# Causal convolution by Karatsuba products: input transposes moved from TensorE to DMA, a fourth accumulation pair, products and sums reordered

## Chip, cores, metric

One core of one Trainium2 chip. The metric is the device time of one launch in microseconds; a run's mean granted TensorE clock (the clock that the chip allowed, 1 being full speed) is given where it matters.

## The reference

```python
# x: (8, 4096, 512) float32, kernel: (8, 512, 512) float32
for k in range(8):
    shifted = x if k == 0 else concat([zeros(B, k, D), x[:, :-k, :]], axis=1)
    out += matmul(shifted, kernel[k])
```

Eight taps, each a 512 x 512 matrix. The kernel splits time in groups of eight and applies a Karatsuba-like scheme three times over: 27 products of a 128 x 512 by 512 x 512 matrix take the place of 64 for each iteration of eight time steps, at the price of sums of inputs (on VectorE) and of results. There are 32 such iterations.

## The kernel before

Each iteration has three nodes, MID, LO and HI, of nine products each. The kernel transposes the input (XT) and loads XT, or sums of it, as the stationary operand (on the page of before, 3,456 weight loads of 128*128 from D and XT). In the profile lines, D stands for the sums and differences of transposed inputs that the prep functions make on VectorE (D1, D2, D4 and so on), pp for an accumulation pair in PSUM, ts and ms for ScalarE's copies of such pairs, y for an output tile.

```python
    xpool = ctx.enter_context(tc.tile_pool(name="x", bufs=2))
    ppool = ctx.enter_context(tc.tile_pool(name="p", bufs=3, space=PSUM))   # accumulation pairs
    tpool = ctx.enter_context(tc.tile_pool(name="t", bufs=2, space=PSUM))   # transposes
    # ... cut ...
    def transpose_x(xin, h, q):                # 8 TensorE transposes and one ScalarE copy
        pt = tpool.tile([P, 2, D], bf, name="pt")
        for j in range(2):
            for c in range(DC):
                nc.tensor.transpose(pt[:, j, c * P:(c + 1) * P],
                                    xin[:, 2 * q + j, c * P:(c + 1) * P], ident)
        nc.scalar.copy(out=XT[:, 4 * h + 2 * q:4 * h + 2 * q + 2, :], in_=pt)
    # ... cut ...
    def node_u(i, a):       # U: one product, then a ScalarE copy within the pair n.q
    def node_a(n):          # A: two products onto n.q, then the ScalarE copy ts
    def node_v(n, b_):      # V: one product to a pair, then the VectorE sum pp with ts
    def node_l(n, b_):      # L: the two last products onto that pair, then ms (ScalarE) or y (VectorE)
    # ... cut: bodies; i is the iteration, a the node, b_ the pair ...
    for k, (i, a) in enumerate(order):
        # ... cut ...
        if a == MID:
            for q in range(2):
                transpose_x(xi[1], 1, q)       # high half of this iteration's input
        if nxt:
            new = node_u(*nxt)
        node_l(cur, 0)
        if nxt:
            node_a(new)
        if a == MID:
            prep_lo_c(); prep_hi_a()           # input sums on VectorE
        elif a == LO:
            prep_d27()
            if not last:
                for q in range(2):
                    transpose_x(xi[0], 0, q)   # low half of the next input
                prep_m()
        elif not last:
            prep_lo_a(); prep_lo_b()
        node_l(cur, 1)
        if nxt:
            node_v(new, 0); node_v(new, 1)
        # ... cut: prep_hi_b, prep_hi_c or prep_d21 ...
```

## Time and profile before

| | before |
|---|---|
| time, median of 7 runs | 1097 us (1094.4 to 1097.9) |
| profiled span, mean clock | 1091.3 us, 0.944 |
| busy TensorE / VectorE / ScalarE | 81% / 73% / 35% |
| start of the first A product | 88.4 us |
| one iteration | 31.25 us |

In 30 of the 31 iterations that have a wait of 2.37 or 2.38 us for D, the granted clock was 0.50 to 0.79 in the 2 us behind it; it was 1.00 behind each of the seven waits for D of 1.13 to 1.24 us.

### The profile page before, as it was taken

The page shows a single profiled execution, that of the slowest core. Times are in us where ns is not written, and L with a number is a line of the kernel's source. Part 1 is how long each engine was busy: PE and PEld are TensorE (multiplying, and loading weights), DVE is VectorE, ACT ScalarE, POOL GpSimd, SP SyncE. Part 2 cuts the span into 40 slices and gives each one's busy share as a digit, 9 for nine tenths or more (in the row PEclk, how much of TensorE's full clock was granted, in tenths as well). Part 3 has the DMA queues.
Part 4 walks back from the last instruction along what each step waited for, and adds up shares of the span by engine and source line. Part 5 has one row for each costly group of instructions (what it writes and reads, how often), then busy time and mean ns, then how long its engine had stood idle before and what let it go on. Part 6 is the DMA issues. An engine that isn't in the chain of part 4 may idle for free. (4 is left out here: it accounts for less than half of the span.)

```text
span 1091.3 us, 11294 instructions
## 1 busy us (share of the span) xinstructions
PE 879.9 (81%) x4432; PEld 406.5 (37%) x4518; DVE 799.4 (73%) x954; ACT 377.5 (35%) x461; POOL 42.9 (4%) x86
## 2 busy tenths in 40 slices
PE   3007888888988888889888888898888888988886
PEld 2003333334443343444333433443334334434342
DVE  2875777777777777787777777877787778777876
ACT  2555233233333233333232333332333333323322
POOL 3000000000000000000000000000000000000000
PEclk9999998999999899999998999999899999989999
DMA  8231343334333433343244233432442334234412
GB/s 207 79 116 39 97 116 98 95 97 116 94 97 100 116 97 97 96 116 88 86 116 116 97 97 97 116 92 82 116 116 97 97 97 116 83 91 116 114 73 84
DMA packets 32436, 110.76 MB, mean 101 GB/s; under 512 B 3472, under 2 KB 3472, under 8 KB 32384
## 3 DMA queue, kind: packets, MB, share of 16 engines
q0 software_dynamic: 9728, 34.54, 18.1%
q1 hardware_dynamic: 22656, 75.51, 17.5%
q8 instruction: 35, 0.57, 0.2%
q14 instruction: 17, 0.14, 0.0%
HBM read 77.46 MB, written 67.11 MB: 132 GB/s over the span
## 5 line engine op out<-in xcount | busy, mean ns | idle before, releaser
L186 PE MATMUL pp<-w,D 128*128 128x512 bf16 x3242 | 789.7, 400 | 112.1 <-DVE D L80 98.1
L186 PEld LDWEIGHTS <-D 128*128 128x128 bf16 x3328 | 329.6, 102 | 561.7 <-DVE D L80 139.1
L80 DVE TENSOR_TENSOR pp<-pp,ts 128x1024 f32<-128x1024 f32 x192 | 226.1, 1223 | 86.1 <-PE pp L186 76.7
L80 DVE TENSOR_TENSOR D<-D 128x512 bf16<-128x512 bf16 (+3 forms) x353 | 242.5, 731 | 2.2
L80 DVE TENSOR_TENSOR y<-pp,ms 128x1024 f32<-128x1024 f32 x128 | 156.0, 1219 | 104.1 <-PE pp L186 101.8
L80 DVE TENSOR_TENSOR D<-XT 128x512 bf16<-128x512 bf16 (+3 forms) x226 | 155.1, 722 | 84.0 <-ACT XT L107 84.0
L214 ACT COPY ts<-pp 128x1024 f32<-128x1024 f32 x96 | 97.2, 1013 | 341.0 <-PE pp L186 336.6
L107 ACT COPY XT<-pt 128x1024 bf16<-128x1024 bf16 x132 | 127.4, 1019 | 107.3 <-PE pt L105 106.2
L207 ACT COPY pp<-pp 128x512 f32<-128x512 f32 x96 | 55.8, 581 | 155.7 <-PE pp L186 155.7
L186 PE MATMUL pp<-w,XT 128*128 128x512 bf16 x128 | 34.1, 384 | 79.1 <-DVE w L80 54.3
L230 ACT COPY ms<-pp 128x1024 f32<-128x1024 f32 x64 | 64.8, 1013 | 69.7 <-PE pp L186 54.5
L105 PE MATMUL pt<-ident,xin 128*128 128x128 bf16 x1056 | 72.2, 223 | 14.0 <-DMA xin<-in_x_dram 13.4
L105 PEld LDWEIGHTS <-xin 128*128 128x128 bf16 x1056 | 66.5, 100 | 29.6 <-issue 13.6
L92 POOL DMA_DIRECT2D xin<-in_x_dram x64 | 33.9, 529 | 984.4 <-PE pt L105 984.4
L186 PEld LDWEIGHTS <-XT 128*128 128x128 bf16 x128 | 12.3, 96 | 85.7 <-issue 73.8
L80 DVE TENSOR_TENSOR mid<-wt 128x1024 f32<-128x1024 f32 (+1 forms) x12 | 18.9, 1574 | 10.0 <-DMA wt<-in_kernel_dram 10.0
L176 ACT CAST w<-mid 128x512 bf16<-128x512 f32 x20 | 12.1, 605 | 25.6 <-DVE mid L80 25.6
L80 DVE TENSOR_TENSOR w<-mid 128x512 bf16<-128x512 f32 x20 | 13.1, 688 | 0.4
L177 ACT ACTIVATE w<-mid 128x512 bf16<-128x512 f32 x20 | 12.5, 625 | 0.0
L80 DVE TENSOR_TENSOR w<-wt 128x512 bf16<-128x512 f32 x16 | 10.3, 683 | 0.0
L177 ACT ACTIVATE w<-wt 128x512 bf16<-128x512 f32 x16 | 10.0, 624 | 0.0
L176 ACT CAST w<-wt 128x512 bf16<-128x512 f32 x16 | 9.6, 601 | 0.0
(13 smaller groups left out, 21.0 us busy)
## 6 DMA issues: line engine op xcount, KB each, us to landing
out_dram<-y SPq DMA_DIRECT2D x128, 512.0 KB, 2.6
xin<-in_x_dram POOLq DMA_DIRECT2D x64, 512.0 KB, 5.0
wt<-in_kernel_dram SPq DMA_DIRECT2D x8, 1024.0 KB, 4.9
xin<-in_x_dram POOLq DMA_DIRECT2D x16, 60.0 KB, 6.7
```

Of the source, the lines that this page charges most:

```text
L80: nc.vector.tensor_tensor(out=o, in0=a, in1=b, op=op)
L92: nc.gpsimd.dma_start(out=xin, in_=xr[:, K * i + 4 * h:K * i + 4 * h + 4, :])
L105: nc.tensor.transpose(pt[:, j, c * P:(c + 1) * P], xin[:, 2 * q + j, c * P:(c + 1) * P], ident)
L107: nc.scalar.copy(out=XT[:, 4 * h + 2 * q:4 * h + 2 * q + 2, :], in_=pt)
L176: nc.scalar.copy(out=W[a, b_, LO][:, c], in_=V[:, 1])
L177: nc.scalar.mul(out=W[a, b_, HI][:, c], in_=V[:, 0], mul=-1.0)
L186: nc.tensor.matmul(bank, lhsT=comp[:, c * P:(c + 1) * P], rhs=w[:, c, :], start=start and c == 0, stop=c == DC - 1, skip_group_check=True)
L207: nc.scalar.copy(out=n.q[:, 0], in_=n.q[:, 1])
L214: nc.scalar.copy(out=n.ts, in_=n.q)
L230: nc.scalar.copy(out=ms[b_], in_=p)
```

## The change

The intent: take the transposes off TensorE and off PSUM. The two PSUM tiles that they held (pt, two of 128x1024 bf16) go, a fourth pair of accumulators (pp, 128x1024 f32) comes, and with four pairs the first product of a node can be issued two nodes ahead. Sums move one slot earlier, and the transposes are issued long before their readers.

```diff
-    ppool = ctx.enter_context(tc.tile_pool(name="p", bufs=3, space=PSUM))
-    tpool = ctx.enter_context(tc.tile_pool(name="t", bufs=2, space=PSUM))
+    ppool = ctx.enter_context(tc.tile_pool(name="p", bufs=4, space=PSUM))
...
-    def transpose_x(xin, h, q):
-        (8 transposes, 1 copy)
+    def transpose_x(xin, h):
+        nc.sync.dma_start_transpose(
+            out=XT[:, 4 * h:4 * h + 4, :].rearrange("p j (c m) -> p (j c) m", m=P),
+            in_=xin.rearrange("p j d -> p (j d)"))
...
     xi = [load_x(0, 0), load_x(0, 1)]
-    for q in range(2):
-        transpose_x(xi[0], 0, q)
+    transpose_x(xi[0], 0)
     prep_m()
-    prep_lo_a()
-    prep_lo_b()
+    prep_d4(LO)
     prep_d21()
+    prep_d41_d42(LO)
+    transpose_x(xi[1], 1)
+    prep_d4(HI)
+    xi = [load_x(1, 0), load_x(1, 1)]
     (the weights' loads and sums follow here, as before)
...
     for k, (i, a) in enumerate(order):          # new order, written out
+        if a == MID and not last:
+            transpose_x(xi[0], 0)
+        node_l(cur, 0, LO); node_l(cur, 0, HI); node_e(cur, 0)
+        if nxt: node_a(nxt)
+        MID: prep_d421(LO)   LO: prep_m(), prep_d4(LO)   HI: prep_d21(), prep_d41_d42(LO)
+        if nxt: node_v(nxt, 0); node_v(nxt, 1)
+        MID: prep_d41_d42(HI), prep_d27()   LO: prep_d421(HI)   HI: prep_d4(HI)
+        node_l(cur, 1, LO)
+        if k + 2 < len(order): nodes.append(node_u(*order[k + 2]))
+        node_l(cur, 1, HI); node_e(cur, 1)
+        if a == LO and not last:
+            transpose_x(xi[1], 1)
+            if i + 2 < NIT: xi = [load_x(i + 2, 0), load_x(i + 2, 1)]
```

More of the change, by code (lines that the diff above doesn't have):

```diff
@@ L80, in tt @@
         nc.vector.tensor_tensor(out=o, in0=a, in1=b, op=op)
-    for _ in range(3):
+    for _ in range(4):
         pw = ppool.tile([P, 2, D], f32, name="pp")
@@ L99, in load_x @@
         return xin
-    def transpose_x(xin, h, q):
-        pt = tpool.tile([P, 2, D], bf, name="pt")
-        for j in range(2):
-            for c in range(DC):
-                nc.tensor.transpose(pt[:, j, c * P:(c + 1) * P],
-                                    xin[:, 2 * q + j, c * P:(c + 1) * P], ident)
-        nc.scalar.copy(out=XT[:, 4 * h + 2 * q:4 * h + 2 * q + 2, :], in_=pt)
+    def transpose_x(xin, h):
+        nc.sync.dma_start_transpose(
+            out=XT[:, 4 * h:4 * h + 4, :].rearrange("p j (c m) -> p (j c) m", m=P),
+            in_=xin.rearrange("p j d -> p (j d)"))
     def prep_m():
@@ L117, in prep_d27 @@
         tt(D2[:, 4], XT[:, 5], XT[:, 7], ADD)
-    def prep_lo_a():
-        tt(D4[:, 0:4], XT[:, 4:8], XT[:, 0:4], ADD)
-        tt(D41[:, 0], D4[:, 7], D4[:, 0], SUB)
-        tt(D41[:, 1], D4[:, 0], D4[:, 1], SUB)
-    def prep_lo_b():
-        tt(D42[:, 0:2], D4[:, 6:8], D4[:, 0:2], ADD)
-        tt(D42[:, 2:4], D4[:, 0:2], D4[:, 2:4], ADD)
     def prep_d21():
@@ L130, in prep_d21, with prep_d4, prep_d41_d42, prep_d421 @@
         tt(D21[:, 1:4], D2[:, 0:3], D2[:, 1:4], SUB)
-    def prep_lo_c():
-        tt(D421[:, 0], D42[:, 7], D42[:, 0], SUB)
-        tt(D421[:, 1:4], D42[:, 0:3], D42[:, 1:4], SUB)
-    def prep_hi_a():
-        tt(D4[:, 4:8], XT[:, 0:4], XT[:, 4:8], ADD)
-        tt(D41[:, 2:4], D4[:, 3:5], D4[:, 4:6], SUB)
-    def prep_hi_b():
-        tt(D42[:, 4:8], D4[:, 2:6], D4[:, 4:8], ADD)
-    def prep_hi_c():
-        tt(D421[:, 4:8], D42[:, 3:7], D42[:, 4:8], SUB)
+    def prep_d4(h):
+        a, b = (XT[:, 4:8], XT[:, 0:4]) if h == LO else (XT[:, 0:4], XT[:, 4:8])
+        tt(D4[:, 4 * h:4 * h + 4], a, b, ADD)
+    def prep_d41_d42(h):
+        if h == LO:
+            tt(D41[:, 0], D4[:, 7], D4[:, 0], SUB)
+            tt(D41[:, 1], D4[:, 0], D4[:, 1], SUB)
+            tt(D42[:, 0:2], D4[:, 6:8], D4[:, 0:2], ADD)
+            tt(D42[:, 2:4], D4[:, 0:2], D4[:, 2:4], ADD)
+        else:
+            tt(D41[:, 2:4], D4[:, 3:5], D4[:, 4:6], SUB)
+            tt(D42[:, 4:8], D4[:, 2:6], D4[:, 4:8], ADD)
+    def prep_d421(h):
+        if h == LO:
+            tt(D421[:, 0], D42[:, 7], D42[:, 0], SUB)
+            tt(D421[:, 1:4], D42[:, 0:3], D42[:, 1:4], SUB)
+        else:
+            tt(D421[:, 4:8], D42[:, 3:7], D42[:, 4:8], SUB)
     xi = [load_x(-1, 0), load_x(-1, 1)]
     for h in range(2):
-        for q in range(2):
-            transpose_x(xi[h], h, q)
+        transpose_x(xi[h], h)
     tt(D4[:, 5:8], XT[:, 1:4], XT[:, 5:8], ADD)
@@ L154 @@
     xi = [load_x(0, 0), load_x(0, 1)]
-    for q in range(2):
-        transpose_x(xi[0], 0, q)
+    transpose_x(xi[0], 0)
     prep_m()
-    prep_lo_a()
-    prep_lo_b()
+    prep_d4(LO)
     prep_d21()
+    prep_d41_d42(LO)
+    transpose_x(xi[1], 1)
+    prep_d4(HI)
+    xi = [load_x(1, 0), load_x(1, 1)]
     with tc.tile_pool(name="wt", bufs=1) as tp:
@@ L222, with node_l, node_e @@
     ms = {}
-    def node_l(n, b_):
+    def node_l(n, b_, j):
+        product(n.p[b_][:, j], n.s[3][2 * b_ + j], W[n.a, b_, j], False)
+    def node_e(n, b_):
         p = n.p[b_]
-        product(p[:, 0], n.s[3][2 * b_], W[n.a, b_, LO], False)
-        product(p[:, 1], n.s[3][2 * b_ + 1], W[n.a, b_, HI], False)
         if n.a == MID:
@@ L237 @@
     order = [(i, a) for i in range(NIT) for a in (MID, LO, HI)]
-    cur = node_u(*order[0])
-    node_a(cur)
-    node_v(cur, 0)
-    node_v(cur, 1)
+    nodes = [node_u(*order[0])]
+    node_a(nodes[0])
+    node_v(nodes[0], 0)
+    node_v(nodes[0], 1)
+    nodes.append(node_u(*order[1]))
     for k, (i, a) in enumerate(order):
-        nxt = order[k + 1] if k + 1 < len(order) else None
+        cur = nodes[k]
+        nxt = nodes[k + 1] if k + 1 < len(order) else None
         last = i + 1 == NIT
-        if a == MID:
-            for q in range(2):
-                transpose_x(xi[1], 1, q)
-            if not last:
-                xi = [load_x(i + 1, 0), load_x(i + 1, 1)]
-        if nxt:
-            new = node_u(*nxt)
-        node_l(cur, 0)
-        if nxt:
-            node_a(new)
-        if a == MID:
-            prep_lo_c()
-            prep_hi_a()
-        elif a == LO:
-            prep_d27()
-            if not last:
-                for q in range(2):
-                    transpose_x(xi[0], 0, q)
-                prep_m()
-        elif not last:
-            prep_lo_a()
-            prep_lo_b()
-        node_l(cur, 1)
-        if nxt:
-            node_v(new, 0)
-            node_v(new, 1)
-        if a == MID:
-            prep_hi_b()
-        elif a == LO:
-            prep_hi_c()
+        if a == MID and not last:
+            transpose_x(xi[0], 0)
+        node_l(cur, 0, LO)
+        node_l(cur, 0, HI)
+        node_e(cur, 0)
+        if nxt:
+            node_a(nxt)
+        if a == MID:
+            prep_d421(LO)
+        elif not last and a == LO:
+            prep_m()
+            prep_d4(LO)
         elif not last:
             prep_d21()
+            prep_d41_d42(LO)
         if nxt:
-            cur = new
+            node_v(nxt, 0)
+            node_v(nxt, 1)
+        if a == MID:
+            prep_d41_d42(HI)
+            prep_d27()
+        elif a == LO:
+            prep_d421(HI)
+        elif not last:
+            prep_d4(HI)
+        node_l(cur, 1, LO)
+        if k + 2 < len(order):
+            nodes.append(node_u(*order[k + 2]))
+        node_l(cur, 1, HI)
+        node_e(cur, 1)
+        if a == LO and not last:
+            transpose_x(xi[1], 1)
+            if i + 2 < NIT:
+                xi = [load_x(i + 2, 0), load_x(i + 2, 1)]
 _INS = ['x', 'kernel']
```

## The prediction

The sum came to 906 us of span, 912 timed and 918 said, and its terms stand; the cut landing enters it only through the start, where the 29 us for the weights' request count four DMA transposes, of which the trace of before has none. The 9% for slower counts some 4% for rival 2.

> **What bounds the kernel now.** I read the busy shares first, then the clock row and the groups, then one iteration in the timeline, then the waits. The chain that ended last is of little use here: its pieces start only at 1051 us, so it tells the last 3% of the run.
>
> ```profile
> PE 879.9 (81%) x4432; PEld 406.5 (37%) x4518; DVE 799.4 (73%) x954; ACT 377.5 (35%) x461; POOL 42.9 (4%) x86
> ...
> PEclk9999998999999899999998999999899999989999
> ...
> L186 PE MATMUL pp<-w,D 128*128 128x512 bf16 x3242 | 789.7, 400 | 112.1 <-DVE D L80 98.1
> L80 DVE TENSOR_TENSOR pp<-pp,ts 128x1024 f32<-128x1024 f32 x192 | 226.1, 1223 | 86.1 <-PE pp L186 76.7
> L80 DVE TENSOR_TENSOR y<-pp,ms 128x1024 f32<-128x1024 f32 x128 | 156.0, 1219 | 104.1 <-PE pp L186 101.8
> L107 ACT COPY XT<-pt 128x1024 bf16<-128x1024 bf16 x132 | 127.4, 1019 | 107.3 <-PE pt L105 106.2
> L105 PE MATMUL pt<-ident,xin 128*128 128x128 bf16 x1056 | 72.2, 223 | 14.0 <-DMA xin<-in_x_dram 13.4
> ...
> out_dram<-y SPq DMA_DIRECT2D x128, 512.0 KB, 2.6
> xin<-in_x_dram POOLq DMA_DIRECT2D x64, 512.0 KB, 5.0
> ```
>
> Neither engine is full: TensorE is busy 81%, VectorE 73%, they wait for each other in turn (VectorE's sums before TensorE's products, TensorE's products before VectorE's evictions), and the clock row is below 10 in nearly every slice. The two DMA rows give the time to landing of 512 KB. The timeline shows one iteration's worst place:
>
> ```profile
> 513.94 1.06 PE L105 MATMUL pt<-ident,xin 128*128 128x128 bf16 x16
> ...
> 516.10 1.96 DVE L80 TENSOR_TENSOR D<-XT 128x512 bf16<-128x512 bf16 x4 [2.12 <-ACT XT L107]
> 517.98 1.22 DVE L80 TENSOR_TENSOR y<-pp,ms 128x1024 f32<-128x1024 f32 x1
> ...
> 519.11 2.35 DVE L80 TENSOR_TENSOR pp<-pp,ts 128x1024 f32<-128x1024 f32 x2
> 519.25 1.02 PE L186 MATMUL pp<-w,XT 128*128 128x512 bf16 x4 [0.80 <-DVE y L80]
> ...
> 521.37 1.21 DVE L80 TENSOR_TENSOR D<-D 128x2048 bf16<-128x2048 bf16 x1
> ...
> 522.64 8.39 PE L186 MATMUL pp<-w,D 128*128 128x512 bf16 x32 [2.37 <-DVE D L80]
> 523.05 0.15 PEld L186 LDWEIGHTS <-D 128*128 128x128 bf16 x1 [0.28 <-issue]
> ```
>
> VectorE waits 2.12 us for the transposed input, so the eviction y comes late, so TensorE waits for a free accumulation pair (0.80 us), then for the last sum (2.37 us). After that the weight loads come 0.43 us apart (0.15 + 0.28) instead of 0.216: the clock has fallen to half, for some 6 matmuls here and some 14 in another iteration that I looked at. The waits repeat in each of the 32 iterations:
>
> ```profile
> PE pp L186 <- DVE D L80: 98.1, 63, 3.0
> PE pp L186 <- DVE y L80: 24.8, 31, 0.8
> ```
>
> One iteration takes 31.25 us (the same transposes start at 93.3 us in the first and at 499.6 us in the fourteenth: 406.3 / 13). It splits so: 27 products of 4 matmuls. A warm run of 28 matmuls took 6.22 us with about 0.17 us of draining in it, so 0.216 us each, 0.863 a product, 23.3 an iteration. Transposes: two groups of 16, issued over about 0.9 us each, 1.8. Waits: (98.1 + 24.8) / 32 = 3.8. The rest, about 2.3 us, is the half clock (6 to 14 matmuls lose 0.21 us each). Sum 31.2.
>
> [...] The trace of before has no DMA transpose; its plain 512 KB store lands in 2.6 us. [...]
>
> **The change part by part.** *Removed:* 1,056 transposes on TensorE (1.8 us an iteration, on the path) and 132 copies on ScalarE (127.4 us in all; ScalarE is 35% busy, so it gains nothing itself, but the 2.12 us wait of VectorE goes). *Added:* 66 DMA transposes of 512 KB on the SP queue. *Moved:* the first product of a node is issued two nodes ahead, between the two last products of the current one, and sums go one slot earlier. VectorE's work is the same: 18 sums, 6 pp and 4 y per iteration. So the floors are TensorE 23.3 us and VectorE about 23.4 us (the mean busy time in three stretches of 31.3 us is 23.49). Both cannot be met, since they still hand over to each other, so I walk the new order of each engine with measured times. Back to back, VectorE takes 1.14 for pp or y (two pp in 2.35), 1.13 for a 2048 sum, 0.87 for 1536, 0.60 for 1024, 0.33 for 512. TensorE to VectorE or ScalarE costs 0.2 after the last matmul's issue end (0.17 drain), the other way 0.06.
>
> Time 0 is the MID node's start. Each node has nine products: two last ones (b=0), A, A, V, V, a last one, U of the node after next, a last one, 7.8 us unstalled. MID has no y, so VectorE has room: its pp end at 7.1, its sums at 9.1. LO starts at 7.8; its first pair is complete at 9.53. From here VectorE has in a row: y 9.73 to 10.87; D1 and D2 (4 sums, 1.87) to 12.74; D4 low 1.13 to 13.87; two pp to 16.14; D421 high 1.13 to 17.27. TensorE has finished LO at 15.6 and needs D421 high for HI: it waits until 17.35, about 1.75 us. HI then runs unstalled to 25.15 (its pp for the next MID end at about 24.7 and 25.8, in time for 25.2 and later). The ring that repeats is 20 products (17.3 us) plus a VectorE segment of 1.14 + 1.87 + 1.13 + 2.27 + 1.13 + 0.26 = 7.8 us, together 25.1 us. Seven products hide under the segment. A stall of 1.75 us amid dense products should not drop the clock, as the present lone waits of 1.1 us do not. So an iteration goes from 31.25 to 25.1 us.
>
> *The fourth pair:* the second V needs the pair that y(b=0) frees, about 1.5 us after its last product while TensorE has three other products, 2.6 us; U takes the pair freed by the ts copy, 2.6 us after A with 1.25 needed. Neither waits. With three pairs this order would.
>
> *The transposes' deadlines:* the low half is issued behind the y store of HI, about 2.9 us into MID, and is needed at 10.87, so it may take 8 us. The high half is issued behind y of LO at 18.4 and is needed by the D4 high sums at 25.8: 7.4 us, and about 1.2 more before VectorE's slack in MID is gone. [...]
>
> *The start:* now the four first transposes stand ahead of the kernel's weights on the SP queue; before, weights were requested at 0.74 us. The fourth must follow both input loads (5.0 us each) and the first D4 sums. I estimate weights requested near 29 us, the first mid4 sum near 36 instead of 29.8: plus 6 us. The later weight chunks keep their period of 15 us. U of the second node adds 0.9. The first MID node thus starts near 93 + 7 = 100 us.
>
> *Sum:* 100 + 31 x 25.1 + 23.4 (the last iteration lacks the next input's sums and so the stall) + 1.4 (last y) + 3.5 (y to span's end, as before) = 906 us. The timed median lies 6 us over the profiled span (1097.25 against 1091.3): 912. A walk by hand meets none of the small delays, so I say 918.
>
> **Rivals.** (1) The transposes are slow, 10 to 15 us each: every us beyond 8 is paid on VectorE's path, for both halves, so 3 to 13 us an iteration: 1,000 to 1,320 us. [...] Against: DMA is busy only about 36% in steady state. [...] (3) VectorE alone becomes the bound, every handover hidden: 23.5 us an iteration, 860 us. Against: the ring above holds TensorE up once per iteration. (4) The waits only move, and the stalls still drop the clock: about 2.5 us more an iteration, 990 us.
>
> **Range and chances.** The walk gives 912, transposes of 8 to 10 us or clock drops carry it to 1,000, better overlap to 885. I say 885 to 1005. Rival 1 in its harder half and rival 2 give the chance of slower, 9%; within 2% is a thin band between, 3%; faster 88%.
>
> **What would show it.** Right: no L105 group; TensorE waiting once per iteration for VectorE's D, 1 to 2 us; clock 0.98 or more; VectorE above 85% busy; [...] period about 25 us; first MID node near 100 us. Wrong: VectorE waiting for XT by DMA for us at a time, SP's issue of one transpose lasting over 8 us, a clock that still falls, or TensorE waiting for freed accumulation pairs.

## The result, and the profile after

The changed kernel took 925.39 us (median of 4 runs, 922.41 to 927.49) against 1096.52 us (4 runs of the same rounds); the ratio is 0.844 (95% interval 0.841 to 0.847). Ratios here are the mean time of one kernel's fast runs over that of the other's fast runs of the same rounds, so they are not quite the quotient of the medians quoted.

The page of the changed kernel, in the same places as before (busy time, clock, groups, DMA issues):

```profile
PE 758.2 (82%) x3464; PEld 336.7 (36%) x3464; DVE 793.2 (86%) x954; ACT 255.9 (28%) x329; POOL 43.0 (5%) x86
...
PEclk9999999999999999999999999999999999999999
...
L181 PE MATMUL pp<-w,D 128*128 128x512 bf16 x3328 | 730.5, 380 | 61.9 <-DVE D L79 53.2
L79 DVE TENSOR_TENSOR pp<-pp,ts 128x1024 f32<-128x1024 f32 x192 | 226.5, 1225 | 26.2 <-ACT ts L209 26.2
L79 DVE TENSOR_TENSOR y<-pp,ms 128x1024 f32<-128x1024 f32 x128 | 156.3, 1221 | 46.4 <-PE pp L181 46.4
L79 DVE TENSOR_TENSOR D<-XT 128x512 bf16<-128x512 bf16 (+3 forms) x226 | 152.5, 722 | 34.0 <-DMA XT<-xin 34.0
...
out_dram<-y SPq DMA_DIRECT2D x128, 512.0 KB, 3.0
...
XT<-xin SPq DMA_TRANSPOSE x66, 5.0
```

The products' matmuls are as many (3,328 + 128 weight loads on both pages; some matmul records of before are missing from its trace) and a little shorter in the mean, 380 ns in place of 400. What went is the transposes' group, the copies from pt, and about half or more of the idle time in front of each row. VectorE does nearly the same work (793 us, before 799) in a shorter span, so its share rose to 86%. A DMA transpose lands after 5.0 us (median), a plain store of the same 512 KB after 3.0.

One iteration in the timeline (start, duration, engine, group, idle time before it and its releaser):

```profile
505.15 1.22 DVE L79 TENSOR_TENSOR y<-pp,ms 128x1024 f32<-128x1024 f32 x1 [0.57 <-PE pp L181]
506.30 3.09 DVE L79 TENSOR_TENSOR D<-XT 128x512 bf16<-128x512 bf16 x5
...
509.30 2.36 DVE L79 TENSOR_TENSOR pp<-pp,ts 128x1024 f32<-128x1024 f32 x2
...
511.57 1.22 DVE L79 TENSOR_TENSOR D<-D 128x2048 bf16<-128x2048 bf16 x1
...
512.84 17.44 PE L181 MATMUL pp<-w,D 128*128 128x512 bf16 x80 [1.68 <-DVE D L79]
514.38 3.28 SPq L101 DMA_TRANSPOSE XT<-xin  x1
...
521.26 1.22 DVE L79 TENSOR_TENSOR D<-XT 128x2048 bf16<-128x2048 bf16 x1
```

This is the predicted ring, piece for piece: y, five sums, two pp, the D421 sum, and then TensorE, which had waited 1.68 us, runs 80 matmuls (20 products) without a pause up to the next y. The chain of waits, which for this kernel covers the whole loop, shows the same 80 matmuls repeating every 25.16 us (start, duration, what; merged pieces of two iterations):

```profile
487.68 17.45 PE pp L181 x80
505.15 1.22 DVE y L79
...
511.57 1.23 DVE D L79
512.84 17.45 PE pp L181 x80
```

The time went as follows. The first MID node's last products began at 118.0 us (worked out: its ms copy starts at 119.93, which is two products of 0.863 and 0.2 of handover later), where before the corresponding point was 93.3: 24.7 us lost at the start. 31 periods of 25.16 in place of 31.25 us: 188.8 us won. From the last MID node to the end 24.9 in place of 29.2 us: 4.3 won. Together 168.4, the difference of the spans (1091.3 and 922.9). Per iteration the 6.1 us are the two groups of transposes (1.8), TensorE's waits for VectorE (from 3.8 to 53.2 / 32 = 1.66, so 2.2) and the rest (about 2.3, all gone), which the prediction called the half clock; the parts are rounded and sum to 6.3. This is an account of TensorE's time, not of what each part would bring by itself. The trace of before bounds the last part: with a mean granted clock of 0.944 over 1091.3 us, the half clock can have cost at most 0.056 x 1091.3 = 61 us, 1.9 an iteration. One iteration of before even ran wholly at full clock (1.00 from 535.97 to 566.17 us, the starts of the same ms copy) and took 30.20 us, 1.05 less than the mean of 31.25; so an estimate of what the half clock was worth is some 1 us of the 6.1.

The start before its first products is where the changed kernel is worse (start, duration and queue of the first transposes and of the weights' requests, and VectorE's first weight sum, which was at 29.82 us before):

```profile
9.23 34.32 SPq L101 DMA_TRANSPOSE XT<-xin  x4
16.36 0.57 POOL L91 DMA_DIRECT2D xin<-in_x_dram  x1 [5.50 <-DMA XT<-xin]
29.05 0.96 DVE L79 TENSOR_TENSOR D<-XT 128x1536 bf16<-128x1536 bf16 x1 [25.76 <-DMA XT<-xin]
...
37.40 3.10 DVE L79 TENSOR_TENSOR D<-XT 128x512 bf16<-128x512 bf16 x5 [6.60 <-DMA XT<-xin]
...
43.60 50.53 SPq L162 DMA_DIRECT2D wt<-in_kernel_dram  x8
45.19 1.23 DVE L79 TENSOR_TENSOR D<-XT 128x2048 bf16<-128x2048 bf16 x1 [1.61 <-DMA XT<-xin]
...
54.16 2.29 DVE L79 TENSOR_TENSOR mid<-wt 128x2048 f32<-128x2048 f32 x1 [7.75 <-DMA wt<-in_kernel_dram]
```

The four transposes and the two input loads between them follow one another, and the weights are requested behind them, at 43.6 us.

### The profile page after: what moved, and what is told of

The parts are those of the page before. It is cut to its first block, busy times and chain, and to the rows that moved or that the text cites. A ratio compares the mean times of both kernels' runs of the same rounds, so it can differ in the third digit from the quotient of the medians.

```text
span 922.9 us, 9305 instructions
## 1 busy us (share of the span) xinstructions
PE 758.2 (82%) x3464; PEld 336.7 (36%) x3464; DVE 793.2 (86%) x954; ACT 255.9 (28%) x329; POOL 43.0 (5%) x86
## 2 busy tenths in 40 slices
DMA packets 169709, 145.25 MB, mean 157 GB/s; under 512 B 140752, under 2 KB 140752, under 8 KB 169664
## 4 chain that ended last, share of the span: by engine, by line
PE 61%; DVE 21%; issue 5%; ACT 0%; DVEq 0%
PE pp L181 61%; DVE D L79 11%; DVE pp L79 7%; DVE y L79 4%; ACT ts L209 0%; DVEq L79 0%; ACT w L172 0%; ACT pp L202 0%
## 5 line engine op out<-in xcount | busy, mean ns | idle before, releaser
L181 PE MATMUL pp<-w,D 128*128 128x512 bf16 x3328 | 730.5, 380 | 61.9 <-DVE D L79 53.2
L181 PEld LDWEIGHTS <-D 128*128 128x128 bf16 x3328 | 323.2, 98 | 479.0 <-DVE D L79 69.0
L79 DVE TENSOR_TENSOR D<-D 128x512 bf16<-128x512 bf16 (+3 forms) x353 | 239.5, 731 | 0.0
L79 DVE TENSOR_TENSOR D<-XT 128x512 bf16<-128x512 bf16 (+3 forms) x226 | 152.5, 722 | 34.0 <-DMA XT<-xin 34.0
L91 POOL DMA_DIRECT2D xin<-in_x_dram x64 | 34.0, 531 | 827.9 <-DMA XT<-xin 827.9
L95 POOL DMA_DIRECT2D xin<-in_x_dram x16 | 8.3, 530 | 1.2 <-DVE xin L93 1.2
L79 DVE TENSOR_TENSOR mid<-mid 128x1024 f32<-128x1024 f32 x4 | 4.9, 1225 | 0.3
L85 PE MATMUL pp<-zero,ident 128*128 128x512 bf16 x8 | 3.6, 630 | 1.4 <-POOL ident masks.py:199 1.4
```

What stands on the lines that cost most here:

```text
L79: nc.vector.tensor_tensor(out=o, in0=a, in1=b, op=op)
L85: nc.tensor.matmul(pw[:, h], lhsT=ident, rhs=zero, start=True, stop=True)
L91: nc.gpsimd.dma_start(out=xin, in_=xr[:, K * i + 4 * h:K * i + 4 * h + 4, :])
L95: nc.gpsimd.dma_start(out=xin[b * G + 1:(b + 1) * G], in_=xr[b * G:(b + 1) * G - 1, RUN - 8 + 4 * h:RUN - 4 + 4 * h, :])
L181: nc.tensor.matmul(bank, lhsT=comp[:, c * P:(c + 1) * P], rhs=w[:, c, :], start=start and c == 0, stop=c == DC - 1, skip_group_check=True)
```

## The experiments

The theory: the period is set by a ring of 20 products on TensorE and a run of VectorE work in LO (y, D1 and D2, D4 low, pp twice, D421 high), and the change lives on the order and on the fourth pair; the DMA is a means, good only while it is issued early. A ring here is a chain of steps, each waiting for the one before, that comes back to its own start one iteration later; its length is then the period. The rivals: that TensorE's freed time is the gain; that the fourth pair, or the interleaving, is it alone; that VectorE's total work is the bound. All ten kernels gave a correct result; each was timed in three rounds beside the kernel before, plus the profiled run (e8 has six runs).

| run | what differs | us (median) | ratio to before | period, us |
|---|---|---|---|---|
| after | the whole change | 925.4 | 0.844 | 25.16 |
| e1_swap | before, transposes by DMA | 1220.0 | 1.112 | 34.8 |
| e2_swap_4pairs | e1 with four pairs | 1217.8 | 1.110 | 34.8 |
| e10_u_back | after, U one node ahead | 926.7 | 0.846 | 25.16 |
| e11_u_back_3pairs | e10 with three pairs | 1207.4 | 1.102 | 34.1 |
| e3_pe_mid | after, 16 matmuls more in MID | 950.2 | 0.866 | 26.06 |
| e4_pe_lo | after, 16 matmuls more at LO's end | 925.9 | 0.843 | 25.16 |
| e5b_d4lo | after, one sum moved out of the ring | 891.6 | 0.813 | 24.03 mostly, mean 24.1 |
| e8_hi_twice | after, high transpose twice | 1004.8 | 0.915 | 27.8 |
| e6_weights_first | after, weights requested first | 915.0 | 0.834 | as after |
| e7_best | LO reordered and new start | 847.9 | 0.773 | 23.86 |

Periods are the distances between the same ms copies of successive iterations (e1, e2 and e11, which vary by up to 2 us: the median; e8: the mean of all 31; e10: between the starts of its 104 matmuls behind the wait).

### e1_swap: the transposes alone

```diff
-        pt = tpool.tile(...); 8 x nc.tensor.transpose(...); nc.scalar.copy(...)
+        nc.sync.dma_start_transpose(out=XT[...], in_=xin...)   # at the same two places
-    tpool = ...
```

> The kernel before with only the transposes swapped for DMA (three pairs, old order). My theory (the gain is in the order, not in TensorE's freed time): the low half is issued behind a y store and used at once, about 7 us after it against 4.2 us through TensorE and ScalarE, so VectorE waits some 3 to 4 us more an iteration, TensorE saves 1.8: period 32 to 34 us against 31.25, start 24 us later, 1,120 to 1,200 us in all. Rival (the transposes on TensorE were the cost): period 29.4 us and 24 us later start, about 1,060 us.

Measured 1220.0 us, 11% slower than before: the rival falls, and the theory's 1,120 to 1,200 was still too low. The timeline of e1_swap shows the low half's wait:

```profile
606.58 0.33 SPq L229 DMA_DIRECT2D out_dram<-y  x1
607.01 3.29 SPq L101 DMA_TRANSPOSE XT<-xin  x1
...
612.04 1.96 DVE L79 TENSOR_TENSOR D<-XT 128x512 bf16<-128x512 bf16 x4 [5.16 <-DMA XT<-xin]
...
615.19 1.87 PE L180 MATMUL pp<-w,XT 128*128 128x512 bf16 x4 [4.73 <-DVE y L79]
...
618.59 8.48 PE L180 MATMUL pp<-w,D 128*128 128x512 bf16 x32 [1.53 <-DVE D L79]
```

VectorE waits 5.16 us for XT where it waited 2.12 for ScalarE's copy (from the start of the y ahead to that reader are 6.7 us, in before 3.7; the expectation's 7 and 4.2 were estimates), the y behind it is late, and TensorE waits 4.73 us for a pair. The clock row of e1_swap stands at 8 tenths in most slices of the loop, where before's is mostly at 9 (mean 0.885 and 0.944), and behind the 4.73 us the weight loads come 0.43 us apart: the clock was lower too, which my expectation had left out. So a plain swap loses, and the 32 x 1.8 us of TensorE time that it frees do not show.

### e2_swap_4pairs: the fourth pair in the old order

```diff
-    ppool = ... bufs=3
+    ppool = ... bufs=4      # on top of e1_swap
```

> As e1_swap with a fourth accumulation pair and still the old order. If the pair itself removes waits, TensorE's 0.8 us wait for a freed pair goes: about 25 us less than e1_swap. My theory: in the old order the pair is only rotation, at most those 25 us and perhaps nothing, since the next wait (for the last sum) takes its place. Rival (the pair is the main gain): within 5% of the changed kernel's 925 us.

1217.8 us, no more than noise away from e1_swap. The waits (who waited for whom: us in total, times, longest) say why. Those of e1_swap:

```profile
DVE D L79 <- DMA XT<-xin: 219.2, 64, 20.0
PE pp L180 <- DVE y L79: 154.2, 44, 6.3
...
PE pp L180 <- DVE D L79: 97.4, 63, 3.0
```

and those of e2_swap_4pairs:

```profile
PE pp L180 <- DVE D L79: 226.5, 63, 5.5
DVE D L79 <- DMA XT<-xin: 223.4, 64, 27.0
...
PE pp L180 <- DMA XT<-xin: 51.4, 31, 2.5
```

With four pairs TensorE no longer waits for y at all, but for the sums D and for XT itself: 277.9 us in place of 251.6. One wait took the place of the other, as VectorE still waits 223 us for the DMA. The pair alone brings nothing.

### e10_u_back and e11_u_back_3pairs: interleaving and the fourth pair in the new order

```diff
         cur = nodes[k]
+        if k + 1 < len(order):
+            nodes.append(node_u(*order[k + 1]))      # U one node ahead, as before
...
-        if k + 2 < len(order):
-            nodes.append(node_u(*order[k + 2]))
```

and for e11 also `bufs=3` in place of 4.

> The changed kernel with the first product U of a node moved back to where it stood before: one node ahead, at the start of a step. Ring theory: U of MID still runs under VectorE's segment (it then stands just ahead of the product that waits), so the ring keeps its 20 products and the period its 25.16 us: 925 us within 1%. Rival (the interleaving of three nodes hides the copy behind U and is worth a wait per node): the copy of 0.57 us and its handover show, 30 us or more.

> As e10_u_back, with three accumulation pairs in place of four (the order with U two nodes ahead needs four live pairs). If the fourth pair is what the change lives on: U at the start of a step waits for the last eviction of the step before it (about 2.9 us in MID and in HI, 1.2 us in LO), and the second V for the ts copy (0.4 us a node): period about 30 to 31.5 us, 1,080 to 1,130 us, most of the gain gone. If the pair is not needed once the sums and transposes are placed so: 925 us.

e10: 926.7 us, the same as after. Interleaving three nodes brings nothing by itself; U stands under the same stretch of VectorE work in both places. e11: 1207.4 us, so the three pairs cost 281 us, more than the 1,080 to 1,130 us that I expected. Its waits:

```profile
PE pp L181 <- DVE y L79: 197.6, 62, 3.3
...
PE pp L181 <- ACT ms L226: 35.2, 32, 1.1
```

TensorE waits for y twice an iteration, for ms once, each time for a freed pair, and 22.6 us in all for the ts copy: 255.4 / 32 = 8.0 us, close to the 8.2 us to which the pieces of my expectation add up (2.9 + 2.9 + 1.2 and 3 x 0.4), though not with the same shares. What it left out is the rest of the 34.1 us over the 23.3 of products, 2.8 us. The half clock is part of that (nine weight loads 0.43 us apart in the iteration that I looked at), by the mean clock of 0.953 over 1206.4 us at most 1.8 us an iteration; the remaining 1.0 us is not explained.

So with DMA transposes and U in its old place, four runs make a square: old placement with three pairs 1220.0, with four 1217.8; new placement of sums and transposes with three pairs 1207.4, with four 926.7. Neither half is worth more than about 1% without the other; together they are worth 293 us.

### e3_pe_mid and e4_pe_lo: what TensorE's time is worth

```diff
+    def idle_transposes(p):                 # 16 matmuls of 128 columns that add zeros
+        for j in range(4):
+            for c in range(DC):
+                nc.tensor.matmul(p[:, 0, c*P:(c+1)*P], lhsT=D4[:, j, c*P:(c+1)*P],
+                                 rhs=zero[:, 0:P], start=False, stop=False, ...)
e3:
+        if a == MID: idle_transposes(cur.p[0])      # ahead of node_l(cur, 0, LO)
e4:
+        if a == LO: idle_transposes(cur.p[1])       # behind node_l(cur, 1, HI)
```

> The changed kernel with 16 extra 128-column matmuls (of zeros, so the result stays right) per iteration at the start of MID, as much TensorE time as one group of the removed transposes, 0.91 us. Ring theory: they lie in the 20 products of the ring, so the period grows by 0.9 us from 25.16 and the total by about 28 us to 953. Rival (TensorE has 1.66 us of waiting an iteration, so that much work is free): 925 us.

> The same 16 extra matmuls at the end of LO, just ahead of TensorE's wait for D421 high. Ring theory: they fill 0.91 of the 1.66 us wait, period and total unchanged, 925 us (within 4 us), TensorE's wait per iteration 0.75 us. Rival (every microsecond on TensorE counts): 953 us.

e3 took 950.2 us with a period of 26.06, 0.90 us longer; e4 took 925.9 with the old 25.16. The timeline of e4_pe_lo shows the extra group filling the wait ahead of HI:

```profile
512.61 1.06 PE L236 MATMUL pp<-zero,D 128*128 128x128 bf16 x16
514.46 13.77 PE L181 MATMUL pp<-w,D 128*128 128x512 bf16 x63 [0.79 <-DVE D L79]
```

In e3_pe_mid the same group lies in the ring and the wait stays:

```profile
505.89 1.06 PE L236 MATMUL pp<-zero,D 128*128 128x128 bf16 x16
506.79 13.98 PE L181 MATMUL pp<-w,D 128*128 128x512 bf16 x64
...
524.17 4.06 PE L181 MATMUL pp<-w,D 128*128 128x512 bf16 x18 [1.68 <-DVE D L79]
```

The same work costs 25 us at one place and nothing at another. So the TensorE time that the change freed would be worth some 25 of the 171 us if one of the two groups lay in the ring; that is argued from e3 and e4, not shown. The new order with the transposes themselves on TensorE was not tried: their PSUM tiles have gone to the fourth pair, and e11 shows what three pairs cost in this order.

### e5b_d4lo: the ring made shorter

```diff
         elif not last and a == LO:
             prep_m()
-            prep_d4(LO)
...
         elif a == LO:
             prep_d421(HI)
+            if not last:
+                prep_d4(LO)
```

> The changed kernel with one sum (D4 low, 1.13 us) moved behind the D421 sum that TensorE waits for. Ring theory: the repeating ring (20 products and a VectorE segment of 7.8 us) gets 1.13 us shorter, period 24.05 against 25.16 us, total about 890 us, and TensorE's wait per iteration 0.5 us against 1.66. Rival (VectorE's total work is the bound): nothing changes, since the same sums run, 925 us.

891.6 us against 925.4, the same sums in another order: the rival of VectorE's total work falls. TensorE's wait is 0.55 us in most iterations, as expected. Timeline of e5b_d4lo:

```profile
445.96 21.76 PE L181 MATMUL pp<-w,D 128*128 128x512 bf16 x100 [0.55 <-DVE D L79]
...
469.99 10.32 PE L181 MATMUL pp<-w,D 128*128 128x512 bf16 x47 [0.55 <-DVE D L79]
```

From one to the next are 24.03 us. But VectorE's wait for the input's DMA begins to show: 8 times in the loop (120 to 870 us), 4.0 us in all, and the iterations that have it take 24.1 to 24.8 us. In the changed kernel all three such waits lie in the start.

### e8_hi_twice: how far the DMA is hidden

```diff
         if a == LO and not last:
             transpose_x(xi[1], 1)
+            transpose_x(xi[1], 1)
```

> The changed kernel with the high half's DMA transpose issued twice in each iteration. If the deadline of the prediction holds (about 7.4 us, some 1.2 us more before it costs) the second one lands 3 to 5 us too late, the D4 high sum, the last y and then the freed pair of MID's first V come late, and the period grows by 2 to 3.5 us: 990 to 1,035 us. Rival (the transposes are hidden with room to spare): 925 to 930 us.

1004.8 us, period 27.8 us on average (25 to 30), within what I expected. Timeline of e8_hi_twice:

```profile
500.01 6.41 SPq L101 DMA_TRANSPOSE XT<-xin  x2
...
509.62 1.23 DVE L79 TENSOR_TENSOR D<-XT 128x2048 bf16<-128x2048 bf16 x1 [2.65 <-DMA XT<-xin]
510.77 1.22 DVE L79 TENSOR_TENSOR y<-pp,ms 128x1024 f32<-128x1024 f32 x1
...
512.04 9.66 PE L181 MATMUL pp<-w,D 128*128 128x512 bf16 x44 [1.32 <-DVE y L79]
```

D4 high is late, so is y, and MID's first V waits for the pair. In the changed kernel the one transpose begins at 514.38 and its reader starts at 521.26 without waiting: it is hidden, with little to spare.

### e6_weights_first: the start

```diff
     xi = [load_x(-1, 0), load_x(-1, 1)]
+    for n in range(3):
+        load_w(n)            # the first three weight loads, ahead of the transposes on SP
```

> The changed kernel with the first three weight loads requested ahead of the four first transposes on the SP queue, nothing else moved. If the late request delays the start: first mid4 sum from 54.2 us to about 43 us, where the chain of input loads and transposes ends that VectorE's order still puts before it; total about 914 us, same period. If the loads only take the transposes' time away: no change, 925 us.

915.0 us. VectorE's first weight sum in e6_weights_first, with no wait before it:

```profile
40.69 1.23 DVE L79 TENSOR_TENSOR D<-XT 128x2048 bf16<-128x2048 bf16 x1 [1.43 <-DMA XT<-xin]
...
41.83 2.29 DVE L79 TENSOR_TENSOR mid<-wt 128x2048 f32<-128x2048 f32 x1
```

It came 12.3 us earlier than after's 54.16, and the span is 11.3 us shorter. What remains ahead of it is the chain of loads and transposes that VectorE's order puts first.

### e7_best: both mends

```diff
         elif a == LO:                     # ahead of the two V and their pp
-            prep_m(); prep_d4(LO)
+            prep_d421(HI); prep_d1()
...
         elif a == LO:                     # behind them
-            prep_d421(HI)
+            prep_d2(); prep_d4(LO)
...
+        for n in range(3): load_w(n)      # start: weights first
         for h in range(2): transpose_x(xi[h], h)
+        chunk(0); load_w(3)               # weight sums of one chunk
         ...                               # sums of the first transposed input
         transpose_x(xi[0], 0)
+        load_w(4); chunk(1); load_w(5)
         prep_d1(); prep_d2(); prep_d4(LO)
         transpose_x(xi[1], 1)
+        load_w(6); chunk(2); load_w(7)
         prep_d21(); prep_d41_d42(LO); prep_d4(HI)
+        chunk(3)
```

> Both mends together: LO's sums in the order D421 high, D1, pp, pp, D2, D4 low, so that no sum for HI stands behind work that nothing waits for, and the weights' first chunk requested and worked on ahead of the input's sums. Ring theory: TensorE's wait in HI goes, VectorE's 23.5 us an iteration and the handover of pp to MID remain, period 23.8 to 24.1 us, 31 x 1.2 = 37 us less or a little more; start about 30 us earlier: 850 to 865 us. If TensorE's wait only moves to another place: about 890 us.

847.9 us (846.59 to 848.4), ratio 0.773, just under the expected 850 to 865: it beats both kernels. Its period is 23.86 us, close to VectorE's 23.5 and to the 23.3 of TensorE's products, so that which of the two engines now holds it is not shown; its first pp starts at 81.51 us, where after's is at 116.71. 35.2 us of start and 31 x 1.30 us of period are 75.5 us, and the spans differ by 76.7 (922.9 and 846.2). Its HI no longer waits for a sum; a wait of 0.39 us for pp is left at MID:

```profile
512.49 13.76 PE L197 MATMUL pp<-w,D 128*128 128x512 bf16 x63 [0.39 <-DVE pp L79]
```

## Why the prediction was right

Predicted 918 us, measured 925.4; the profiled spans were 906 (worked out) and 922.9. The loop was right in its mechanism; that the total came so near has some luck in it, since 12 us of allowances (6 for timed over profiled, of which 2.5 were real, and 6 for small delays) made up for most of a start that was mis-sized by 18 us. By its steps:

- *The ring.* Predicted 20 products and a VectorE segment of 7.8 us, 25.1 us; measured 25.16, with the very pieces named. Changing its length shows the ring: e5b took 1.13 us out of the segment and the period fell by 1.1, e3 put 0.9 us into it and the period grew by 0.90, e4 put the same work beside it and the period stayed.
- *TensorE's wait in HI.* Predicted 1.75 us, measured 1.68.
- *The clock.* Predicted not to fall; the loop runs at full clock (granted 1.00 from 131 to 900 us, with a wait for D of 1.66 us in the mean in each iteration). Two readings of before were off, without touching the walk of the new order: in the clock row a 9 stands for 90% or more, so the row does not show a clock "below 10 in nearly every slice" (five of its 40 slices are under 90%, and the changed kernel's row is all 9 at a mean of 0.999); and the 2.3 us given to the half clock are a remainder of which the trace allows at most 1.9. What does show the half clock are the weight loads 0.43 us apart, with a granted clock of 0.50 from 522.64 to 525 us. (The mean clock of a run is no safe measure: one run of the changed kernel lists 0.942 at 922.41 us, and e5b's clock row is at 5 and 6 tenths only in its idle start.)
- *The fourth pair.* "Neither waits. With three pairs this order would": right, and the size of it (281 us between e10 and e11) is the largest single effect found. That it is worthless in the old order (e2) the prediction did not say.
- *The interleaving.* The prediction put U two nodes ahead among the moved parts without a value; e10 shows that it has none.
- *The transposes' deadlines.* The estimate of the landing is cut; measured are 5.0 us in the median, 4.3 to 7.0 in the loop. In the iteration shown the high half is issued at 514.38 us and read at 521.26, 6.9 us later, the low half is issued at 498.97 and read from 506.30 on, 7.3 us later (7.4 and 8 predicted). Right, with less room than these told.
- *Mis-sized: the start.* "plus 6 us" was wrong in size: the first weight sum came at 54.2 us and not at 36, the first MID node at 118.0 and not at 100. Of the 18 us, 14.6 are the weights' request (43.6 for 29): the first four transposes landed after 7.0 us in the median, up to 12.8, beside the input loads, and stood on the queue one behind the other, for which the 29 us, an estimate without a measured transpose, had too little; 3.6 are the two weight loads, for which I had allowed 7 us and which took 10.6 us. e6 shows that the request's place on the queue is the cause of 12 of them.
- *Mis-sized: the end.* 28.3 us from the last MID node to the end was expected, 24.9 measured: I gave the last LO and HI nodes nine products each, but with no node after next and no next node they have eight and four, 5.2 us less; against that stands a wait of 1.17 us before HI that I had ruled out. The two errors and 31 x 0.06 us of period make 18.0 - 3.4 + 1.9 = 16.5 of the 16.9 us between 906 and 922.9.
- *Timed over profiled.* I added 6 us; it was 2.5. In every run whose span is on record the time is about 1.8 us over it; the 6 set the median of the timed runs against the span of the profiled one, which by this rule ran 4 us faster than that median.

Rival 1 (slow transposes) is real but was not reached: e8 shows what it would have looked like. Rival 2 is cut; one transpose's record on the SP queue lasted 3.24 us in the median (1.3 to 5.3). Rival 3 (VectorE alone as bound) comes close to e7_best, not to the change. Rival 4 (waits move and the clock still falls) is in kind what the new order gives with three pairs, e11 (mean clock 0.953), though that cost far more than its 990 us.

## What to carry to other kernels

Where two engines take turns, write out one period with measured durations and find the ring: here 0.90 us of work in the ring cost 0.90 us a period (e3), the same work beside it nothing (e4), and moving one 1.1 us sum past the one that the other engine waits for was worth 34 us. A transfer put in place of an engine's work has to be issued at least one landing time ahead of its reader (5.0 us in the median here; e1, with 5.0 us from issue to reader, made VectorE wait 5.16), and buffers and order have to change together: with the transposes on DMA, either alone left this kernel 10 to 11% slower than before. Look at the start as well: a queue that serves both a long chain and the loads that everything waits for should serve the loads first (11.3 us of span in e6).

## What the traces show of the DMA transpose

- A 512 KB transpose within SBUF landed after 5.0 us in the median, where a plain store of the same size took 3.0 in the same run. The packets of queue q1 (hardware_dynamic) took 17.5% of the 16 engines' 1091.3 us before and 44.0% of 922.9 after: 215 us more for 66 transposes, 3.26 us each, an estimate of 161 GB/s (it counts what the stores lost beside them).
- The count of packets under 512 B rose from 3,472 to 140,752, 2,080 for each of 66 transposes of 512 KB: in the trace 2,048 of exactly 256 B, which are the 512 KB, and 32 of 4 B.
- A transpose's record on SP lasted 3.24 us in the median (1.3 to 5.3), a plain store's 0.33 (0.33 to 0.58). With 1.3 us at the least it is no fixed time.
- The landing differs with the stretch: 7.0 us in the median of the first four, with input loads in flight, and up to 12.8 us, against 4.3 to 7.0 us in the loop.
